# Quartered first loads, high parts kept in PSUM and a paired first output tile in a hybrid decoder step

## The chip, the cores and the metric

The kernel runs on one core of a Trainium2 chip. The metric is the device time of one execution in microseconds (us). Before the change it is 1032.31 us, the median of three runs (1032.12 to 1032.55). Engines are named as in the profile: PE is TensorE (PEld its weight loads), DVE is VectorE, ACT is ScalarE, POOL is GpSimd, SP is SyncE, which here only issues transfers.

## The reference, cut to what matters

One layer of a decoder for 512 prompt rows and 32 sample rows, in float32, D = 1024. The parts around the change:

```
mod = silu(c) @ w_ada + b_ada;  sh1, sc1, g1, sh2, sc2, g2 = split(mod, 6)
u = x * (1 + sc1) + sh1
a = u @ w_in + b_in                       # columns: convolution branch (GLU), q, k, v, two gates
y_conv = conv_branch(glu(a)) ;  y_att = attention(a) @ w_pa + b_pa
y = (gate_c * y_conv + gate_a * y_att) @ w_out + b_out
x = layer_norm(ALPHA * x + (1 + g1) * y, ln1_g, ln1_b)
u = x * (1 + sc2) + sh2 ;  h = (silu(u @ w_gate) * (u @ w_up)) @ w_down
x = layer_norm(ALPHA * x + (1 + g2) * h, ln2_g, ln2_b)
```

c, and so mod, is one vector for the prompt and one for each of 8 sample sequences. The key and value windows and the convolution state are outputs too.

## The kernel before, in words

All 544 columns (512 prompt, 32 sample) stand in the free dimension, in two halves of HC = 272; D lies on the partitions in 8 blocks k. Every float32 product is made of three: an operand is split into a high part (a cast to fp32r, by ACT) and a low part (source minus high, by DVE), and PE adds hi·hi, hi·lo and lo·hi in PSUM. `mm_group` (lines 193 to 205) does this for one 128-column weight tile: 8 blocks x 2 halves x 3 = 48 matmuls of 272 columns, or 24 for one half or for 4 blocks. Its PSUM tiles come from `pmm`, which has four.

Weight tiles come as a stream in a fixed order. `load_more` (L110 to L119) issues their transfers from SP as long as one of four raw buffers `wr` is free; `prep_to` (L121 to L138) splits them (ACT at L133, DVE at L134) into one of three buffers `wh` and `wl`; `w_next` keeps that three tiles ahead of PE. The order on each engine is the order in which the program is written; background generators advance at `tick()`.

**Load phase** (L206 to L321). SP loads the modulation weights `ga` in four groups g of 2 MiB (two transfers each), x in two, and whole tiles of `w_in` in between; ACT loads `ct`, `cst` and `vec`. For each g, `ada_mm(g)` makes the part of sh1 and sc1 that belongs to the blocks k = 2g and 2g + 1 (32 matmuls), `make_u(g)` transposes it, makes modT (DVE, L267) and from it the two blocks of u, split (ACT L274 and L246, DVE L275, L277 and L247, POOL L279 and L280). `early_mm(g)` adds those two blocks' share into the first NE = 3 projection tiles, 36 matmuls, 12 per tile. The written order is product 0, u 0, product 1, u 1, early 0, product 2, u 2, early 1, product 3, u 3, early 2, early 3; the three tiles are split whole in between. Then `mm_group` runs for the further tiles, from 47.2 us.

**Modulation for the rest** (`ada_gen`, L326 to L361): eight blocks `gb` of `w_ada`, loaded by POOL with `ada_load`, are used one after each projection group, the first behind the group m = 3.

**Merge** (L826 to L850). For each of the 8 blocks m, PE makes att @ w_pa (24 matmuls); DVE adds the bias and multiplies by the gate, half by half (L836); for m < DM = 7 POOL adds the convolution branch `t1` (L845), and the split of that block into M is done one step later by `merge_split`; for m = 7 DVE adds (L838) and the split follows at once:

```
act.copy(out=M[h][:, 0, m], in_=mg[:, h * HC:(h + 1) * HC])
dve.tensor_tensor(out=M[h][:, 1, m], in0=mg[:, ...], in1=M[h][:, 0, m].bitcast(F32), op=ALU.subtract)
```

**Output projection and first layer norm** (L980 to L1008). For half h = 0 and then 1, and for the 8 blocks m, `mm_group` multiplies M[h] by `w_out` tile m (`wo`), and DVE adds the result, times 1 + g1, into z (L992). z is x, loaded again by SP (L853); ahead of that first use POOL scales all of it by ALPHA and adds (1 + g1)·b_out (`xbb`) in eight instructions of 512 columns and one for the samples (L989, L991). `Stats` adds sums (DVE) and squares (ACT, added by POOL) as the blocks come; `ln1_gen(h)` finishes the norm between the next matmul groups.

Of the kernel before, what the change touches and what calls it, by code (L numbers as in the profile page):

```python
# [7 lines left out]
F32 = mybir.dt.float32  # L8
# [9 lines left out]
NP = 512  # L18
# [36 lines left out]
def hybrid_step_kernel(ctx: ExitStack, tc: tile.TileContext, I, O):  # L55
# [156 lines left out]
    x_sb = big_tile(2, [128, 8, NT], F32, "x_sb")  # L212
    act.dma_start(out=cst[:, :128], in_=I["cst"][:, :128])
    act.dma_start(out=vec, in_=I["vec"])
    ga = []
    for g in range(4):
        t = big_tile(3 + g, [128, 8, 512], F32, f"ga{g}")
        for i in range(2):
            sp.dma_start(out=t[:, 4 * i:4 * i + 4], in_=I["w_ada0"][g, :, 4 * i:4 * i + 4])
        if g % 2 == 0:  # L220
            sp.dma_start(out=x_sb[:, 2 * g:2 * g + 4], in_=I["x_t"][:, 2 * g:2 * g + 4])
        if g < 2:
            load_more(1 + 2 * g)
        ga.append(t)
    load_more()
    act.dma_start(out=cst[:, 128:], in_=I["cst"][:, 128:])
    dve.memset(cpad, 0.0)
    dve.memset(ones, 1.0)
    dve.memset(epst, EPS)
    pool.memset(smv, 0.0)  # L230
    ident = C("ident")
# [48 lines left out]
        pool.tensor_tensor(out=samp(us), in0=samp(us), in1=bc(modT[:, 0, ks, 1:9]), op=ALU.add)  # L280
        split_samp(us, U[1], ks)

    NE = 3
    early = [[(pmm if m < 2 else ps_s).tile([128, 512], F32, tag="mm" if m < 2 else "s", name="mm") for _ in range(2)] for m in range(NE)]
    ew = []

    def early_mm(g):
        for m in range(NE):
            hi, lo = ew[m]
            for k in (2 * g, 2 * g + 1):  # L290
                for h in range(2):
# [6 lines left out]
    a0 = ada_mm(0)
    make_u(0, a0)
    prep_to(1)  # L300
    a1 = ada_mm(1)
    prep_to(2)
    make_u(1, a1)
    prep_to(3)
    for m in range(NE):
        ew.append(preps.pop(m))
    pos["use"] = NE
    early_mm(0)
    a2 = ada_mm(2)
    make_u(2, a2)  # L310
    early_mm(1)
    a3 = ada_mm(3)
    make_u(3, a3)
    early_mm(2)
    dve.tensor_scalar(out=qb, in0=V("b_in", 0, 60), scalar1=0.125, scalar2=None, op0=ALU.mult)


    aslots = (3, 4, 5, 6, 3, 4, 6, 4)
    abox = {}

    def ada_load(c):  # L321
        t = big_tile(aslots[c], [128, 2, 2048], F32, f"gb{c}")
        pool.dma_start(out=t, in_=I["w_ada12"][c])
        abox[c] = t

    def ada_gen():  # L326
# [35 lines left out]
    glu_p = glu[:, :4 * 542].rearrange("p (c t) -> p c t", c=4)  # L362
    glu_s = glu[:, 4 * 542:4 * 542 + 4 * NB * 34].rearrange("p (c b t) -> p c b t", c=4, b=NB)
    ctmp = glu[:, 4 * 542 + 4 * NB * 34:].rearrange("p (b t w) -> p b t w", b=NB, w=CW)
    for c in range(4):
        ada_load(c)
    pool.memset(glu_p[:, :, 0:30], 0.0)
    for c in range(4):
        pool.dma_start(out=glu_s[:, c, :, 0:30], in_=I["state"][:, c])
# [455 lines left out]


    def merge_split(m, mg, h):
        act.copy(out=M[h][:, 0, m], in_=mg[:, h * HC:(h + 1) * HC])
        dve.tensor_tensor(out=M[h][:, 1, m], in0=mg[:, h * HC:(h + 1) * HC], in1=M[h][:, 0, m].bitcast(F32), op=ALU.subtract)  # L829

    for m in range(8):
        ps = mm_group(w_next(), att, 4)
# [146 lines left out]
    for h in range(2):  # L979
        stats = Stats(h, dve)  # L980
        for m in range(8):
            if h == 0:
                wo.append(w_next())
            ps = mm_group(wo[m], M, 8, halves=(h,))[h]
            n1 = HC if h == 0 else 240
            zz = stats.zt(m)
            if h == 0 and m == 0:
                for k in range(8):
                    pool.tensor_scalar(out=z[:, k, :NP], in0=z[:, k, :NP], scalar1=ALPHA, scalar2=xbb[:, k:k + 1], op0=ALU.mult, op1=ALU.add)  # L989
                prep_to(pos["use"] + XP)  # L990
# [510 lines left out]
```

## Time and profile before

| | before |
|---|---|
| median of three runs | 1032.31 us (1032.12 to 1032.55) |
| the profiled execution | 1033.35 us |
| its span, first to last instruction | 1031.6 us |
| mean granted PE clock | 0.986 |
| PE / PEld busy | 985.8 us (96%) / 942.2 us (91%) |
| DVE / ACT / POOL busy | 652.1 us (63%) / 479.7 us (47%) / 236.3 us (23%) |
| moved by DMA | 242.64 MB, mean 235 GB/s |

The page gives busy times by engine and by 40 slices of the span; matmuls are pipelined, so a busy PE is not PE at its peak, and start-to-start distances tell more than single durations. Further views: stretches (busy time of each engine between two times, with the granted clock and the DMA engines' share), the timeline (instructions in order of time, with the idle time before them and what ended it), lines or tiles (min, median and max of one kind of instruction), the list of waits, and the DMA view.

### The profile page before, as it was taken

Reading aid. Unit: us, or ns where it says so; the run is one execution under the profiler, and the core shown is the slowest. Engines: PE = TensorE matmul, PEld = TensorE weight load, DVE = VectorE, ACT = ScalarE, POOL = GpSimd, SP = SyncE. Lnnn points to the kernel's source line nnn. Section 1 sums busy time; section 2 is a strip of 40 time slices with the busy share of each in tenths; the row PEclk is TensorE's granted clock in tenths of the full one; section 3 lists DMA queues with packets and bytes.
Section 4 is the critical chain, followed back from the end, with each engine's and each line's share of the span. In section 5 each row is a group of like instructions: output and inputs, shape, how many; then the busy total and the mean of one; then the engine's idle time right before and its main releaser. Section 6 shows DMA issues by size and latency. Waiting matters only on the chain.

```text
span 1031.6 us, 21539 instructions
## 1 busy us (share of the span) xinstructions
PE 985.8 (96%) x8964; PEld 942.2 (91%) x8964; DVE 652.1 (63%) x1156; ACT 479.7 (47%) x931; POOL 236.3 (23%) x279
## 2 busy tenths in 40 slices
PE   4999999999999999999999998989999999999995
PEld 3887999999998999999999998989999999999994
DVE  3422788879886654342217887687546875578687
ACT  3312235545447667534433445656325652266333
POOL 0301010010013310101103444054014440344046
PEclk8999999999999999999999998999999999999998
DMA  9998687696784674699953620124964769565612
GB/s 379 361 385 319 244 298 261 246 339 233 277 324 163 238 271 154 236 378 384 367 202 99 242 83 21 42 83 170 349 255 162 266 209 360 205 246 207 213 50 86
DMA packets 44945, 242.64 MB, mean 235 GB/s; under 512 B 7408, under 2 KB 10736, under 8 KB 37680
## 3 DMA queue, kind: packets, MB, share of 16 engines
q1 hardware_dynamic: 34592, 126.83, 34.4%
q10 hardware_dynamic: 7632, 88.43, 23.0%
q0 software_dynamic: 2624, 26.02, 6.3%
q8 instruction: 70, 1.15, 0.4%
q14 instruction: 27, 0.22, 0.1%
HBM read 231.36 MB, written 97.58 MB: 319 GB/s over the span
## 4 chain that ended last, share of the span: by engine, by line
PE 61%; DVE 12%; issue 8%; ACT 7%; POOL 6%; DMA 5%; ACTq 0%; DVEq 0%; POOLq 0%
PE mm L199 15%; PE mm L200 14%; PE mm L202 14%; POOL ss L1077 4%; DMA wr<-in_w_gu 3%; PE od L740 2%; PE mm L1120 2%; PE Sd L705 2%; PE mm L1121 2%; PE mm L1122 2%; PE adaps L334 1%; DVE mrg L829 1%; DMA wr<-in_w_in 1%; PE pt L516 1%; DVE wl L134 1%
## 5 line engine op out<-in xcount | busy, mean ns | idle before, releaser
L199 PE MATMUL mm<-u,wh 128*128 128x272 f32 x1016 | 283.4, 296 | 1.2 <-ACT wh L133 0.9
L200 PE MATMUL mm<-u,wh 128*128 128x272 f32 x1016 | 275.6, 289 | 0.0
L202 PE MATMUL mm<-u,wl 128*128 128x272 f32 x1016 | 213.2, 290 | 1.3 <-DVE wl L134 1.2
L199 PEld LDWEIGHTS mm<-u,wh 128*128 128x128 f32 x1016 | 192.4, 189 | 15.8 <-issue 11.4
L200 PEld LDWEIGHTS mm<-u,wh 128*128 128x128 f32 x1016 | 192.7, 190 | 0.3
L134 DVE TENSOR_TENSOR wl<-wr,wh 128x1024 fp32r<-128x1024 f32 (+2 forms) x100 | 117.5, 1176 | 86.5 <-ACT wh L133 86.5
L202 PEld LDWEIGHTS mm<-u,wl 128*128 128x128 f32 x1016 | 160.4, 189 | 1.9 <-DVE wl L134 1.9
L133 ACT CAST wh<-wr 128x1024 fp32r<-128x1024 f32 (+2 forms) x100 | 97.0, 972 | 64.6 <-PE mm L200 50.5
L439 DVE SCALAR_TENSOR_TENSOR convy<-glu,vec,convy 128x512 f32<-128x512 f32 x120 | 95.7, 797 | 2.5
L1077 POOL TENSOR_TENSOR ss<-wr 128x512 f32<-128x512 f32 x34 | 50.6, 1487 | 189.3 <-DVE s L1104 85.9
L200 PE MATMUL mm<-h,wh 128*128 128x272 f32 x240 | 64.7, 288 | 0.0
L199 PE MATMUL mm<-h,wh 128*128 128x272 f32 x240 | 64.5, 286 | 0.0
L1034 DVE SCALAR_TENSOR_TENSOR z<-mm,modT,z 128x272 f32<-128x272 f32 (+1 forms) x48 | 21.7, 479 | 49.0 <-PE mm L202 49.0
L637 ACT ACTIVATE qk<-mm,vec 128x272 f32<-128x272 f32 (+1 forms) x48 | 25.9, 627 | 56.5 <-PE mm L202 56.5
L202 PE MATMUL mm<-h,wl 128*128 128x272 f32 x240 | 49.6, 288 | 0.0
L1093 ACT CAST wh<-ss 128x512 fp32r<-128x512 f32 (+1 forms) x34 | 28.4, 835 | 42.8 <-POOL ss L1077 32.1
L199 PEld LDWEIGHTS mm<-h,wh 128*128 128x128 f32 x240 | 45.2, 188 | 0.0
L200 PEld LDWEIGHTS mm<-h,wh 128*128 128x128 f32 x240 | 45.1, 188 | 0.0
L1120 PE MATMUL mm<-ta,wh 128*128 128x272 f32 x136 | 40.4, 297 | 4.6 <-DVE wg L1142 4.6
L509 ACT ACTIVATE P<-P,st 128x256 f32<-128x256 f32 x64 | 31.2, 488 | 28.2 <-DVE st L503 25.7
L654 POOL DMA_DIRECT2D out_kv<-qk x4 | 2.4, 597 | 182.5 <-ACT qk L637 182.5
L200 PE MATMUL mm<-mrg,wo 128*128 128x272 f32 x128 | 37.8, 296 | 1.8 <-DVE mrg L829 1.7
(329 smaller groups left out, 2545.4 us busy)
## 6 DMA issues: line engine op xcount, KB each, us to landing
out_s<-in_c ACTq DMA_DIRECT2D x32, 2044.0 KB, 10.4
wr<-in_w_in SPq DMA_DIRECT2D x60, 512.0 KB, 6.6
wr<-in_w_gu SPq DMA_DIRECT2D x44, 512.0 KB, 3.8
KT<-in_kt SPq DMA_DIRECT2D x24, 792.0 KB, 7.9
VV<-in_vv SPq DMA_DIRECT2D x24, 768.0 KB, 7.8
gb<-in_w_ada POOLq DMA_DIRECT2D x8, 2048.0 KB, 16.9
out_s<-in_c ACTq DMA_DIRECT2D x8, 2032.0 KB, 10.1
ga<-in_w_ada SPq DMA_DIRECT2D x8, 1024.0 KB, 14.3
```

What stands on the lines that cost most here:

```text
L133: act.copy(out=hv, in_=raw)
L134: dve.tensor_tensor(out=lv, in0=raw, in1=hv.bitcast(F32), op=ALU.subtract)
L199: pe.matmul(ps[h][:, :HC], lhsT=hi[:, k], rhs=A[h][:, 0, k], start=(k == 0), stop=False)
L200: pe.matmul(ps[h][:, :HC], lhsT=hi[:, k], rhs=A[h][:, 1, k], start=False, stop=False)
L202: pe.matmul(ps[h][:, :HC], lhsT=lo[:, k], rhs=A[h][:, 0, k], start=False, stop=(k == nk - 1))
L439: dve.scalar_tensor_tensor(out=o, in0=src, scalar=sc, in1=o, op0=ALU.mult, op1=ALU.add)
L509: act.activation(out=p[:, a:b], in_=p[:, a:b], func=AF.Exp, bias=st[:, kd, s, hh, 0:1], accum_out=st[:, kd, s, hh, 1:2])
L637: act.activation(out=o, in_=src, func=AF.Identity, bias=V("b_in", col))
L1034: dve.scalar_tensor_tensor(out=zz[:, :n1], in0=ps[:, :n1], scalar=modT[:, 5, m, 0:1], in1=zz[:, :n1], op0=ALU.mult, op1=ALU.add)
L1077: pool.tensor_tensor(out=o, in0=x, in1=y, op=op)
L1093: act.copy(out=hi, in_=src_of(f, n))
L1120: pe.matmul(ps[:, :HC], lhsT=hi[:, k], rhs=B[:, 0, k], start=(first and k == 0), stop=False, skip_group_check=not first)
```

## The change

1. **Load phase.** x comes in four transfers and the first three `w_in` tiles in quarters (two blocks k each), so that SP loads for each g: `ga`, x, three quarters. The quarters are split one by one (`prep_quarters`), and the early matmuls are spread: `early_mm` takes a list of tiles. Twelve, later six matmuls of `ones` by `ones` (`warm`) are put ahead. The rest of `cst` is loaded by SP behind these.
2. **Modulation for the rest.** Its first four `gb` are loaded by SP instead of POOL, two at once and two behind the groups m = 3 and 4; the products start one group later.
3. **Merge.** For m < 7 ACT copies the high part once more, into a PSUM tile (`mhi`), and DVE subtracts that copy.
4. **Output projection.** The first two tiles of half 0 share one loop: blocks k = 0 to 5 of both, then 6 and 7 of both. z is scaled by ACT block by block, one block ahead of its use, instead of by POOL at once.

```diff
+    def ga_load(g):
+        for i in range(2):
+            sp.dma_start(out=ga[g][:, 4 * i:4 * i + 4], in_=I["w_ada0"][g, :, 4 * i:4 * i + 4])
+    def x_load(g):
+        sp.dma_start(out=x_sb[:, 2 * g:2 * g + 2], in_=I["x_t"][:, 2 * g:2 * g + 2])
+    def w_quarters(g):
+        for m in range(NE):
+            sp.dma_start(out=eraw[m][:, 2 * g:2 * g + 2], in_=stream[m][0][:, 2 * g:2 * g + 2])
+    NE = 3
+    eraw = [wrp.tile([128, 8, 128], F32, tag="wr", name="wr") for _ in range(NE)]
     for g in range(4):
...
+        ga_load(g)
+        x_load(g)
+        w_quarters(g)
+    pos.update(load=NE, prep=NE, use=NE)
     load_more()
-    act.dma_start(out=cst[:, 128:], in_=I["cst"][:, 128:])
+    sp.dma_start(out=cst[:, 128:], in_=I["cst"][:, 128:])
...
+    def warm(n):
+        t = ps_t.tile([128, 128], F32, tag="t", name="warm")
+        for _ in range(n):
+            pe.matmul(t, lhsT=ones, rhs=ones, start=True, stop=True)
+    def prep_quarters(g):
+        ks = slice(2 * g, 2 * g + 2)
         for m in range(NE):
+            hi, lo = ew[m]
+            act.copy(out=hi[:, ks], in_=eraw[m][:, ks])
+            dve.tensor_tensor(out=lo[:, ks], in0=eraw[m][:, ks], in1=hi[:, ks].bitcast(F32), op=ALU.subtract)
+            done[m] = g == 3
+        load_more()
...
+    warm(12)
+    make_u(0, ada_mm(0))
+    prep_quarters(0)
+    warm(6)
+    early_mm(0, (0, 1))
+    make_u(1, ada_mm(1))
+    prep_quarters(1)
+    early_mm(0, (2,))
+    early_mm(1, (0,))
+    make_u(2, ada_mm(2))
+    prep_quarters(2)
+    early_mm(1, (1, 2))
+    early_mm(2, (0,))
+    make_u(3, ada_mm(3))
+    prep_quarters(3)
+    early_mm(2, (1, 2))
...
-    for c in range(4):
-        ada_load(c)
+    for c in range(2):
+        ada_load(c, sp)
...
-        next(ada12, None)
+        if m > NE:
+            next(ada12, None)
+        if m < NE + 2:
+            ada_load(m - NE + 2, sp)
...
     def merge_split(m, mg, h):
+        hi = M[h][:, 0, m].bitcast(F32)
         act.copy(out=M[h][:, 0, m], in_=mg[:, h * HC:(h + 1) * HC])
-        dve.tensor_tensor(out=M[h][:, 1, m], in0=mg[:, h * HC:(h + 1) * HC], in1=M[h][:, 0, m].bitcast(F32), op=ALU.subtract)
+        if m < DM:
+            seen = ps_s.tile([128, 512], F32, tag="s", name="mhi")[:, :HC]
+            act.copy(out=seen, in_=hi)
+            hi = seen
+        dve.tensor_tensor(out=M[h][:, 1, m], in0=mg[:, h * HC:(h + 1) * HC], in1=hi, op=ALU.subtract)
...
-            if h == 0:
+            if h == 0 and m == 0:
+                wo.extend((w_next(), w_next()))
+                pair = [pmm.tile([128, 512], F32, tag="mm", name="mm") for _ in range(2)]
+                for ks in (range(6), (6, 7)):
+                    for i in range(2):
+                        for k in ks:
+                            pe.matmul(pair[i][:, :HC], lhsT=wo[i][0][:, k], rhs=M[0][:, 0, k], start=(k == 0), stop=False)
+                            pe.matmul(pair[i][:, :HC], lhsT=wo[i][0][:, k], rhs=M[0][:, 1, k], start=False, stop=False)
+                            pe.matmul(pair[i][:, :HC], lhsT=wo[i][1][:, k], rhs=M[0][:, 0, k], start=False, stop=(k == 7))
+            elif h == 0 and m > 1:
                 wo.append(w_next())
...
-            if h == 0 and m == 0:
-                for k in range(8):
-                    pool.tensor_scalar(out=z[:, k, :NP], in0=z[:, k, :NP], scalar1=ALPHA, scalar2=xbb[:, k:k + 1], op0=ALU.mult, op1=ALU.add)
-                prep_to(pos["use"] + XP)
-                pool.tensor_scalar(out=z[:, :, NP:], in0=z[:, :, NP:], scalar1=ALPHA, scalar2=None, op0=ALU.mult)
+            if h == 0 and m < 7:
+                for k in ((0, 1) if m == 0 else (m + 1,)):
+                    act.activation(out=z[:, k, :NP], in_=z[:, k, :NP], func=AF.Identity, scale=ALPHA, bias=xbb[:, k:k + 1])
+            if h == 0 and m == 6:
+                act.activation(out=z[:, :, NP:], in_=z[:, :, NP:], func=AF.Copy, scale=ALPHA)
```

How it moves instructions, at three places. On SP at the start of the program (`ga` modulation weights, `wr` raw weight tiles, `gb` the later modulation weights, `cst` constants), before:

```order
L219 DMA ga_111<-in_w_ada 128x2048 x2
L221 DMA x_sb<-in_x_t 128x2176
L117 DMA wr<-in_w_in 128x1024
L219 DMA ga_117<-in_w_ada 128x2048 x2
L117 DMA wr<-in_w_in 128x1024 x2
L219 DMA ga_124<-in_w_ada 128x2048 x2
L221 DMA x_sb<-in_x_t 128x2176
L219 DMA ga_128<-in_w_ada 128x2048 x2
L117 DMA wr<-in_w_in 128x1024 x26
```

and now:

```order
L219 DMA ga_111<-in_w_ada 128x2048 x2
L222 DMA x_sb<-in_x_t 128x1088
L226 DMA wr<-in_w_in 128x256 x3
L219 DMA ga_112<-in_w_ada 128x2048 x2
L222 DMA x_sb<-in_x_t 128x1088
L226 DMA wr<-in_w_in 128x256 x3
L117 DMA wr<-in_w_in 128x1024
L236 DMA cst<-in_cst 128x940
L346 DMA gb_549<-in_w_ada 128x4096
L117 DMA wr<-in_w_in 128x1024 x3
L346 DMA gb_551<-in_w_ada 128x4096
```

The tiles that SP loaded whole now come in three pieces behind each group of `ga` and x (the second and third such groups, which read alike, are left out here), the constants have come over from ACT, and two blocks of `gb` stand ahead of and among the next weight tiles.

On ACT in the load phase, from one copy of a modulation product (`modsb`) to the next (`u` the split input, `wh` high parts of weights), before:

```order
L262 COPY modsb<-adaps 128x128
L274 ACTIVATE u_140<-x_sb,modT 128x272
L274 ACTIVATE u_141<-x_sb,modT 128x240
L246 CAST u_141<-us 128x2x32
L133 CAST wh<-wr 128x1024 x2
L262 COPY modsb<-adaps 128x128
```

and now:

```order
L272 COPY modsb<-adaps 128x128
L284 ACTIVATE u_151<-x_sb,modT 128x272
L284 ACTIVATE u_152<-x_sb,modT 128x240
L256 CAST u_152<-us 128x2x32
L306 CAST wh<-wr 128x256 x3
L272 COPY modsb<-adaps 128x128
```

The two whole tiles split ahead of the next product (of the four parts of u two are shown) have become three quarters, and this now repeats for each of the four groups.

On ACT at the end of the merge (`mrg` the high parts of M, `mhi` their copies in PSUM, `wo` the output projection's weights, `lnq` squares of the layer norm), before:

```order
L133 CAST wo_6346<-wr 128x1024
L828 CAST mrg_6348<-mg 128x272
L828 CAST mrg_6349<-mg 128x272
L828 CAST mrg_6348<-mg 128x272
L828 CAST mrg_6349<-mg 128x272
L133 CAST wo_6346<-wr 128x1024 x2
L133 CAST wo_6681<-wr 128x1024 x3
L898 ACTIVATE lnq<-z 128x272
```

and now:

```order
L133 CAST wo_6395<-wr 128x1024
L855 CAST mrg_6397<-mg 128x272
L858 COPY mhi<-mrg_6397 128x272
L855 CAST mrg_6398<-mg 128x272
L858 COPY mhi<-mrg_6398 128x272
L855 CAST mrg_6397<-mg 128x272
L855 CAST mrg_6398<-mg 128x272
L133 CAST wo_6395<-wr 128x1024 x2
L1029 ACTIVATE z<-z,xbb 128x512 x3
L133 CAST wo_6758<-wr 128x1024
L1029 ACTIVATE z<-z,xbb 128x512
```

Each deferred split has a copy behind its cast, and the scaling of z, which POOL did in one run, stands among the casts of the `w_out` tiles. On PE the first 48 matmuls of the output projection stay neighbours; the blocks 6 and 7 of the first tile now come behind blocks 0 to 5 of the second.

## Rows read from the trace of the kernel before

**Rows 1.** Stretches of the load phase: us, busy of each engine (x count), PEclk, DMA share, GB/s.

```profile
16.50:23.00 6.50, 5.38 (x71) 4.40 (x72) 1.70 (x5) 1.47 (x3) 0.22 (x1) 0.50 1.03 417
...
28.40:47.20 18.80, 17.92 (x240) 17.21 (x239) 8.18 (x23) 6.78 (x15) 7.76 (x13) 1.00 0.87 339
```

**Rows 2.** Timeline, load phase: start us, us, engine, line, what, xcount [idle before <-releaser].

```profile
8.46 1.22 PEld L256 LDWEIGHTS adaps<-ga,cpad 128*32 128x32 f32 x32 [0.47 <-DMA ga<-in_w_ada]
...
11.84 0.26 DVE L267 SCALAR_TENSOR_TENSOR modT<-modt,vec 128x18 f32<-128x18 f32 x2 [5.38 <-DMA vec<-in_vec]
...
16.57 1.94 PE L256 MATMUL adaps<-ga,cpad 128*32 128x128 f32 x32 [5.89 <-DMA ga<-in_w_ada]
...
18.97 1.94 PE L256 MATMUL adaps<-ga,cpad 128*32 128x128 f32 x32 [0.47 <-DMA ga<-in_w_ada]
```

**Rows 3.** Timeline of PE at the first output projection groups.

```profile
569.90 0.29 PE L199 MATMUL mm<-mrg,wo 128*128 128x272 f32 x1
...
572.18 0.29 PE L199 MATMUL mm<-mrg,wo 128*128 128x272 f32 x1
...
574.19 0.39 PE L200 MATMUL mm<-mrg,wo 128*128 128x272 f32 x1 [1.73 <-DVE mrg L829]
...
582.81 0.29 PE L199 MATMUL mm<-mrg,wo 128*128 128x272 f32 x1
```

**Rows 4.** Stretches behind the merge and in the first layer norm.

```profile
576.00:579.40 3.40, 3.40 (x17) 3.40 (x16) 2.68 (x3) 3.40 (x5) 1.51 (x1) 0.50 1.02 397
...
635.30:640.90 5.60, 5.60 (x26) 5.48 (x25) 5.42 (x7) 0.82 (x2) 4.57 (x5) 0.51 0.37 97
```

**Rows 5.** List of waits, PE, 545 to 660 us: us in total, times, longest.

```profile
PE lnps L924 <- DVE lns L881: 1.7, 1, 1.7
PE lnps L925 <- POOL lnq L882: 1.5, 1, 1.5
```

**Rows 6.** DMA view, 0 to 36 us: queue, kind: packets, MB, share of 16 engines.

```profile
q1 hardware_dynamic: 2147, 13.22, 90.8%
...
q10 hardware_dynamic: 576, 0.74, 5.6%
```

**Rows 7.** Timeline, load phase, from the second modT to the end.

```profile
22.45 0.25 DVE L267 SCALAR_TENSOR_TENSOR modT<-modt,vec 128x18 f32<-128x18 f32 x2
...
22.74 2.08 ACT L274 ACTIVATE u<-x_sb,modT 128x272 fp32r<-128x272 f32 x4 [1.30 <-DVE modT L267]
...
25.52 0.22 DVE L247 TENSOR_TENSOR u<-us,u 128x64 fp32r<-128x64 f32 x1
...
28.42 1.95 PE L256 MATMUL adaps<-ga,cpad 128*32 128x128 f32 x64
...
31.18 0.26 DVE L267 SCALAR_TENSOR_TENSOR modT<-modt,vec 128x18 f32<-128x18 f32 x2 [4.02 <-PE modt L264]
...
46.94 0.42 PE L296 MATMUL mm<-u,wl 128*128 128x272 f32 x2
```

**Rows 8.** The merge's tile and line L133: ns min/median/max, first and last start us, forms.

```profile
L828 ACT CAST mrg<-mg x16: 413/418/423, 551.7 to 575.8; 128x272 fp32r<-128x272 f32 x16
...
L829 DVE TENSOR_TENSOR mrg<-mg,mrg x16: 423/436/1608, 552.8 to 576.2; 128x272 fp32r<-128x272 f32 x16
...
L133 ACT CAST wh<-wr x100: 602/1044/1094, 14.2 to 957.9; 128x1024 fp32r<-128x1024 f32 x76, 128x512 fp32r<-128x512 f32 x16, 128x896 fp32r<-128x896 f32 x8
```

**Rows 9.** Timeline of DVE at the end of the merge.

```profile
568.99 0.90 DVE L836 SCALAR_TENSOR_TENSOR mg<-mm,vec,ga 128x272 f32<-128x272 f32 x2
...
572.82 0.49 DVE L836 SCALAR_TENSOR_TENSOR mg<-mm,vec,ga 128x272 f32<-128x272 f32 x1
...
577.16 2.36 DVE L134 TENSOR_TENSOR wo<-wr,wo 128x1024 fp32r<-128x1024 f32 x2 [0.50 <-ACT wo L133]
```

**Rows 10.** Line L1104, its second operand in SBUF or in PSUM (`hip`).

```profile
L1104 DVE TENSOR_TENSOR wl<-wr,wh x37: 677/684/1782, 677.7 to 953.5; 128x512 fp32r<-128x512 f32 x37
...
L1104 DVE TENSOR_TENSOR wl<-ss,hip x14: 686/687/690, 692.2 to 945.6; 128x512 fp32r<-128x512 f32 x14
```

More of the change, by code (lines that the diff above doesn't have):

```diff
@@ L214, in hybrid_step_kernel @@
     act.dma_start(out=vec, in_=I["vec"])
-    ga = []
-    for g in range(4):
[L217 to L224, printed above, removed]
+    ga = [big_tile(3 + g, [128, 8, 512], F32, f"ga{g}") for g in range(4)]
+    def ga_load(g):
[8 more added lines that the diff above has]
+    eraw = [wrp.tile([128, 8, 128], F32, tag="wr", name="wr") for _ in range(NE)]
+    for g in range(4):
+        ga_load(g)
+        x_load(g)
+        w_quarters(g)
+    pos.update(load=NE, prep=NE, use=NE)
     load_more()
-    act.dma_start(out=cst[:, 128:], in_=I["cst"][:, 128:])
+    sp.dma_start(out=cst[:, 128:], in_=I["cst"][:, 128:])
+    dve.memset(ones, 1.0)
     dve.memset(cpad, 0.0)
-    dve.memset(ones, 1.0)
     dve.memset(epst, EPS)
@@ L281, in make_u, with early_mm @@
         split_samp(us, U[1], ks)
-    NE = 3
     early = [[(pmm if m < 2 else ps_s).tile([128, 512], F32, tag="mm" if m < 2 else "s", name="mm") for _ in range(2)] for m in range(NE)]
-    ew = []
-    def early_mm(g):
-        for m in range(NE):
+    def warm(n):
+        t = ps_t.tile([128, 128], F32, tag="t", name="warm")
+        for _ in range(n):
+            pe.matmul(t, lhsT=ones, rhs=ones, start=True, stop=True)
+    ew = [(whp.tile([128, 8, 128], F32R, tag="wh", name="wh"), wlp.tile([128, 8, 128], F32R, tag="wl", name="wl")) for _ in range(NE)]
+    def prep_quarters(g):
+        ks = slice(2 * g, 2 * g + 2)
+        for m in range(NE):
+            hi, lo = ew[m]
[3 more added lines that the diff above has]
+        load_more()
+    def early_mm(g, ms=range(NE)):
+        for m in ms:
             hi, lo = ew[m]
@@ L296, in early_mm @@
                     pe.matmul(early[m][h][:, :HC], lhsT=lo[:, k], rhs=U[h][:, 0, k], start=False, stop=(k == 7))
[L298 to L314, printed above, removed]
+    warm(12)
[14 more added lines that the diff above has]
+    early_mm(2, (1, 2))
     dve.tensor_scalar(out=qb, in0=V("b_in", 0, 60), scalar1=0.125, scalar2=None, op0=ALU.mult)
@@ L319, in hybrid_step_kernel, with ada_load @@
     abox = {}
-    def ada_load(c):
+    def ada_load(c, eng=pool):
         t = big_tile(aslots[c], [128, 2, 2048], F32, f"gb{c}")
-        pool.dma_start(out=t, in_=I["w_ada12"][c])
+        eng.dma_start(out=t, in_=I["w_ada12"][c])
         abox[c] = t
@@ L981, in hybrid_step_kernel @@
         for m in range(8):
-            if h == 0:
+            if h == 0 and m == 0:
[8 more added lines that the diff above has]
+            elif h == 0 and m > 1:
                 wo.append(w_next())
-            ps = mm_group(wo[m], M, 8, halves=(h,))[h]
+            ps = pair[m] if h == 0 and m < 2 else mm_group(wo[m], M, 8, halves=(h,))[h]
             n1 = HC if h == 0 else 240
             zz = stats.zt(m)
-            if h == 0 and m == 0:
-                for k in range(8):
-                    pool.tensor_scalar(out=z[:, k, :NP], in0=z[:, k, :NP], scalar1=ALPHA, scalar2=xbb[:, k:k + 1], op0=ALU.mult, op1=ALU.add)
-                prep_to(pos["use"] + XP)
-                pool.tensor_scalar(out=z[:, :, NP:], in0=z[:, :, NP:], scalar1=ALPHA, scalar2=None, op0=ALU.mult)
+            if h == 0 and m < 7:
[3 more added lines that the diff above has]
+                act.activation(out=z[:, :, NP:], in_=z[:, :, NP:], func=AF.Copy, scale=ALPHA)
             dve.scalar_tensor_tensor(out=zz[:, :n1], in0=ps[:, :n1], scalar=modT[:, 2, m, 0:1], in1=zz[:, :n1],
```

## The prediction

> **What bounds the kernel now.** [...]
>
> The first is the load phase, up to the first full projection group at 47.2 us. From 16.5 to 23.0 us PE is granted 0.50 of its clock while the DMA engines are full; from 28.4 to 47.2 it has no gap to speak of [rows 1]. The reader should see in the timeline what it waited for: the second modulation product sat idle 5.89 us for its weights, its second half came at 18.97, and before that the first modT waited until 11.84 for `vec` [rows 2]. So by 28.4 us little of the three early tiles was done, and the rest had to be worked off after the loads.
>
> The second is the step from the merge to the output projection. PE starts the first `w_out` group at 569.90, issues 18 matmuls, starts the 19th at 572.18 and the 20th only at 574.19; the fourth group starts at 582.81 [rows 3]. From 576.0 to 579.4 the granted clock is 0.50 [rows 4], behind that stall. [...]
>
> After that PE waits twice in the first layer norm, 1.7 us on DVE and 1.5 us on POOL [rows 5], and runs at 0.51 from 635.3 to 640.9 [rows 4]. The change does not address that.
>
> **Load phase: bytes.** A quarter is 2.10 MB of modulation weights, 0.56 MB of x and three pieces of 0.13 MB. Anchor: when the second `ga` ended at 18.97 [rows 2], 6.57 MB had been asked for (two `ga`, half of x, one weight tile, the constants), and the engines moved 0.417 MB per us [rows 1]. In the new order the second `ga` is complete at 5.4 MB, so about 16.2; the third at 8.45 MB, 23.5; the fourth at 11.5 MB, 30.8. Small packets cost more per byte: the queue with short rows spent 5.6% of 16 engines and 36 us on 576 packets, 56 ns each for 1.3 KB, the other 244 ns for 6.2 KB [rows 6]. By these, 1536 packets of 1 KB take some 5.4 us against 3.9 for the same bytes in long rows; I put the fourth `ga` at 31.3 us (30.8 to 32.3).
>
> **Load phase: the chain.** Each quarter now runs modT, U, the quarters' split, early matmuls, next modulation product. From modT at 22.45: ACT's four parts of U end at 24.82, the cast of the sample columns 0.23 behind, one copy of 128x256 about 0.42 (the 128x272 cast of [rows 8]), so the first high part stands at +2.95; DVE's last low part of U ends at 25.74, and one low part of 0.44 behind it stands at +3.7 [rows 7]. PE does four of the twelve matmuls meanwhile and the other eight in 1.0: +4.75. From the start of a modulation product to the next modT is 31.18 - 28.42 = 2.76 [rows 7]. Cycle: 7.5 us.
> Without the wait for `vec` the first modT could come at 10.5 (the second half of the first product ends at 8.46 + 1.22, and the way to modT behind a product is 2.76 - 1.95 = 0.8), with it at 11.84 as before [rows 2, 7]; the x transfer beside which `vec`'s rows are dealt has half the packet length now, so I take 10.9. The first quarter does two tiles, 20 matmuls behind +3.7: +6.25, next modT 10.9 + 6.25 + 2.76 = 19.9, then 27.4 and 34.9. Its products need `ga` at 17.2, 24.6 and 32.1: just behind the arrivals. Behind the last modT come 24 matmuls of the third quarter (3.05), then 36: high part in place, low part at +3.7, 32 left at 0.127: +7.8, 42.7 us. Before it was 47.2: 4.5 us gained at full clock.
> That PE is at full clock at 13.9 us is not sure. Warm-up matmuls (12, then 6) stand where PE was idle, up to 6.5 us. A modulation product is 32 matmuls, four side by side, in 1.95 [rows 7], 0.24 for each four; a warm-up moves as many columns, so it costs 0.24, or 0.49 at the lower level, and 12 are done before the product can start. In the trace PE began at 6.5; the 32 weight loads that began at 8.46 took 1.22, where 64 take 1.69 at full clock, so the level rose some 2.8 us after the first work; on the second occasion, from 16.6, it had not risen by 23.0 [rows 1, 2, 7]. I take 2.8 us: from 13.85 to 16.65 twelve matmuls at 0.227 instead of 0.127, 1.1 us lost. **Term: 3.4 us** (bounds: 4.7 with `vec` early and full clock throughout; 1.8 if the level rises 6.4 us after 13.85).
> At nothing, with cover: `cst` to SP's tail (first used in attention); the later modulation loads, which now stand in SP's queue among the weight tiles. The fourth to sixth weight tiles are issued behind 2.1 MB only when the last quarter is split (38.6 us), land at 42 to 45 and are first needed 6 us behind 42.7; the modulation product c = 0 moves one group later. If that cover went, PE would wait for what is missing, 1.2 us per late tile.
>
> **Merge and output projection.** DVE lags: the seventh group's eviction starts at 568.99, the last at 572.82, 3.83 apart, where PE delivers every 24 x 0.127 = 3.04 [rows 9]. In each step one of the two subtractions takes 1608 ns instead of 436, because both operands lie in SBUF while POOL adds [rows 8]. With the high part in PSUM the subtraction took 687 for 512 elements, with both in SBUF 684 at the median but up to 1782; the former ran beside POOL's adds of the same line's operands, and none took more than 690 [rows 10]. So 1.17 us of waiting go, but the weight split that follows still reads SBUF twice and meets the rest of POOL's add, some 0.8: each step gets 0.3 to 0.4 shorter. Steps with 4-block weights then keep up with PE; the two with `w_out` splits do not. The last eviction comes 1.9 us earlier by this; I take 1.5 (bounds 0 and 2.9, the whole lag).
> ACT pays 14 copies of 0.42: with two casts of 0.42 and a weight cast of 1.04 that is 2.7 us in a step of 3.04 [rows 8], nothing on the path.
> [...]
> PE: the first six blocks of two tiles are 36 matmuls, 569.90 to 574.5; the stalled low part is then there (574.19 before, earlier now), the last twelve end at 576.0. No stall, so no fall of the clock. The third tile's low part was ready at 577.16 + 1.2 = 578.4 [rows 9], now 576.9: PE does two matmuls and waits 0.7; 22 x 0.127 later the third group ends at 579.7 where it ended at 582.81. **Term: 3.1 us** (bounds 1.6, DVE no earlier, and 3.75, no wait).
> z's prescale leaves POOL for ACT: eight activations of 0.6 to 1.04 (ACT's four parts of U take 2.08 for 1024 elements with scale and bias [rows 7]), one per group of 3.04 us, beside a cast of 1.04 [rows 8]: at nothing. POOL's prescale had no one waiting on PE's side. If ACT came late, the squares for the layer norm would be late next.
>
> **Sum.** 3.4 + 3.1 = 6.5. The profiled execution took 1033.35 us for a span of 1031.6: 1026.85. It lies 1.04 above the median 1032.31, so I forecast 1032.3 - 6.5 = 1025.8; the two terms' bounds give 1023.9 to 1028.9.
>
> **The rivals.**
> *The gain at the merge is waited away in the layer norm.* PE's waits there name DVE and POOL [rows 5]; were that chain bound by its own work, PE would come 3.1 us earlier and wait 3.1 us longer: 1028.9. Against: before 582.8 DVE waits for PE's groups, so the chain moves with them.
> *The level stays at half to 23 us, as now.* Then 24 matmuls cost 5.45, the second modulation product 1.75 more, the end is 46.7: 0.5 + 3.1, 1028.7. For: the gaps between early matmuls remain. Against: PE works from 1 us on.
> *The half-clock stretch at 635 goes too.* 5.6 us at half cost 2.8: 1023.0.
> *It does nothing:* PE's in-order queue makes each product wait for the split of the quarter before, and the arrivals slip: 1031 to 1032.3.
> *Slower:* one mechanism, PE's level in the load phase. Its work is now spread thinly over 40 us; if every gap keeps it at half, the cycle is 3.7 + 1.8 + 4.7 = 10.2, with 5.45 instead of 3.05 for the 24 matmuls of one quarter and 8.2 for the last 36 the phase ends near 60 instead of 47.2: 12.8 - 3.1 = 9.7 slower, 1042. It is slower than before once 44% of the phase (42.7 to 60.0, break-even 50.3) is at half. For: the level fell after one short burst [rows 1, 2]. Against: at half PE would hardly idle.
> [...]
>
> **How the numbers follow.** Forecast with its bounds 0.55; layer norm 0.14; half to 23 us 0.10; stretch at 635 goes 0.08; nothing 0.08; slower 0.05. The range 1023.0 to 1029.5 takes in the first four, 0.87. A measurement of this kernel tells 0.2%, 2.1 us, from no change: faster 0.87, same 0.08, slower 0.05.
>
> **What would show it.** Right: first full group at 43 to 45 us; modT at about 11, 21, 28 and 36; subtractions of the merge all near 0.44; no matmul of the first pair waiting; granted clock 1.00 from 570 to 630; a wait under 1 us at the third `w_out` tile. Wrong: that group at 47 or later, a clock of 0.50 past 20 us, PE's waits in the layer norm grown by 3 us, or `ga` named as what PE waits for at 30 us.

## The result, and the profile after

The changed kernel took 1026.32 us in the median of 4 runs (1025.97 to 1026.41) beside 1032.43 us for the kernel before (median of 4, 1032.12 to 1034.87): ratio 0.9929, 95% interval 0.9914 to 0.9944. By the medians that is 6.1 us less where 6.5 were forecast. The profiled execution took 1026.41 us for a span of 1024.2, against 1033.35 and 1031.6.

**Load phase.** The stretches view of after, columns as in [rows 1]:

```profile
8.50:16.00 7.50, 5.42 (x62) 4.61 (x63) 4.05 (x12) 3.40 (x9) 0.66 (x2) 1.00 1.04 407
16.00:23.00 7.00, 5.22 (x89) 4.58 (x88) 2.96 (x9) 3.17 (x9) 0.66 (x2) 1.00 1.02 407
```

The granted clock is 1.00 where [rows 1] had 0.50. The timeline of PE, load phase of after:

```profile
1.06 4.69 PE L298 MATMUL warm<-ones 128*128 128x128 f32 x24 [1.06 <-DVE ones L237]
...
8.58 1.08 PE L266 MATMUL adaps<-ga,cpad 128*32 128x128 f32 x32 [0.88 <-DMA ga<-in_w_ada]
...
22.67 0.39 PE L317 MATMUL mm<-u,wh 128*128 128x272 f32 x1 [1.39 <-ACT wh L306]
...
32.33 1.95 PE L266 MATMUL adaps<-ga,cpad 128*32 128x128 f32 x64
...
42.92 0.29 PE L199 MATMUL mm<-u,wh 128*128 128x272 f32 x1
```

The 5.89 us for the second `ga` [rows 2] are gone, and the last modulation product (32.33) waits for nothing. The first full group starts at 42.92, 4.28 earlier. The modT rows of DVE's timeline set the beat:

```profile
10.70 0.26 DVE L277 SCALAR_TENSOR_TENSOR modT<-modt,vec 128x18 f32<-128x18 f32 x2 [4.14 <-DMA vec<-in_vec]
...
19.80 0.26 DVE L277 SCALAR_TENSOR_TENSOR modT<-modt,vec 128x18 f32<-128x18 f32 x2 [4.81 <-PE modt L274]
...
27.44 0.26 DVE L277 SCALAR_TENSOR_TENSOR modT<-modt,vec 128x18 f32<-128x18 f32 x2 [3.34 <-PE modt L274]
...
35.09 0.26 DVE L277 SCALAR_TENSOR_TENSOR modT<-modt,vec 128x18 f32<-128x18 f32 x2 [3.35 <-PE modt L274]
```

Not all of the 4.28 us lasts: at 380.46 in before, 376.51 in after, the same transposes of `fb` are 3.95 apart. PE's timeline shows one of the takers, which before had not:

```profile
79.45 1.92 PE L357 MATMUL adaps<-gb,cpad 128*32 128x512 f32 x16 [0.21 <-DMA gb<-in_w_ada]
```

**Merge and output projection.** The same view, later:

```profile
565.95 0.29 PE L1019 MATMUL mm<-mrg,wo 128*128 128x272 f32 x1
...
571.99 0.29 PE L199 MATMUL mm<-mrg,wo 128*128 128x272 f32 x1
572.12 0.29 PE L200 MATMUL mm<-mrg,wo 128*128 128x272 f32 x1
572.54 0.40 PE L202 MATMUL mm<-mrg,wo 128*128 128x272 f32 x1
...
575.43 0.29 PE L199 MATMUL mm<-mrg,wo 128*128 128x272 f32 x1
```

The pair's 48 matmuls run through. The third tile waits for its low weights: two starts 0.42 apart instead of 0.127, so 0.3 us. The fourth group starts 582.81 - 575.43 = 7.38 us earlier than before [rows 3], the first 569.90 - 565.95 = 3.95: the merge gives 3.43. DVE, in the tile view and the timeline:

```profile
L860 DVE TENSOR_TENSOR mrg<-mg,mhi x14: 422/430/439, 548.9 to 568.2; 128x272 fp32r<-128x272 f32 x14
```

```profile
554.03 0.91 DVE L867 SCALAR_TENSOR_TENSOR mg<-mm,vec,ga 128x272 f32<-128x272 f32 x2
554.85 0.78 DVE L860 TENSOR_TENSOR mrg<-mg,mhi 128x272 fp32r<-128x272 f32 x2
555.70 1.31 DVE L134 TENSOR_TENSOR wl<-wr,wh 128x512 fp32r<-128x512 f32 x1
557.03 0.91 DVE L867 SCALAR_TENSOR_TENSOR mg<-mm,vec,ga 128x272 f32<-128x272 f32 x2
...
566.92 0.49 DVE L867 SCALAR_TENSOR_TENSOR mg<-mm,vec,ga 128x272 f32<-128x272 f32 x1
```

No deferred subtraction takes 1608 ns any more [rows 8]. The weight split takes the wait in its place (1.31 us), and the step, from one L867 to the next, is 3.00 us, PE's own. Only the two steps with splits of `w_out` tiles are longer, 3.46 and 3.43 us. The last eviction starts 0.97 us behind the first output matmul, before 2.92 [rows 3, 9].

**Layer norm.** The list of waits, PE, 560 to 665 us, and the stretches that run at half clock in after:

```profile
PE lnps L955 <- DVE lns L912: 1.7, 1, 1.7
PE lnps L956 <- POOL lnq L913: 1.5, 1, 1.5
PE mm L199 <- ACT wh L133: 1.2, 1, 1.2
```

```profile
308.60:311.90 3.30, 3.30 (x14) 3.07 (x14) 1.81 (x3) 1.44 (x6) 0.00 (x0) 0.50 0.77 248
626.00:632.80 6.80, 5.54 (x22) 5.31 (x23) 5.34 (x6) 2.34 (x5) 5.14 (x5) 0.50 0.28 80
687.50:690.80 3.30, 3.30 (x16) 3.30 (x15) 2.83 (x6) 1.54 (x4) 0.00 (x0) 0.50 0.08 22
```

Both waits are those of [rows 5], and the stretch of [rows 4] is there, with 0.50 from 625.99 on instead of 633.99. The other two are not in the trace of before.

### The profile page after: what moved, and what is told of

It reads as the page before. It is cut to its first block, busy times and chain, and to the rows that moved or that the text cites. A ratio compares the mean times of both kernels' runs of the same rounds, so it can differ in the third digit from the quotient of the medians.

```text
span 1024.2 us, 21677 instructions
## 1 busy us (share of the span) xinstructions
PE 990.5 (97%) x9000; PEld 947.0 (92%) x9000; DVE 651.1 (64%) x1165; ACT 492.3 (48%) x963; POOL 221.7 (22%) x266
## 4 chain that ended last, share of the span: by engine, by line
PE 59%; DVE 12%; ACT 8%; issue 8%; DMA 7%; POOL 5%; ACTq 0%; POOLq 0%; DVEq 0%; SPq 0%
PE mm L199 14%; PE mm L200 14%; PE mm L202 13%; POOL ss L1117 3%; DMA wr<-in_w_gu 3%; DMA gb<-in_w_ada 3%; PE mm L1160 2%; PE mm L1162 2%; PE mm L1161 2%; PE od L766 2%; PE Sd L731 2%; DVE wl L134 1%; PE pt L542 1%; PE adaps L357 1%; DMA wr<-in_w_in 1%
## 5 line engine op out<-in xcount | busy, mean ns | idle before, releaser
L133 ACT CAST wh<-wr 128x1024 fp32r<-128x1024 f32 (+2 forms) x97 | 93.9, 969 | 53.8 <-PE mm L200 42.7
L1162 PE MATMUL mm<-ta,wl 128*128 128x272 f32 x136 | 39.5, 290 | 0.0
```

Of the source, the lines that this page charges most:

```text
L133: act.copy(out=hv, in_=raw)
L1162: pe.matmul(ps[:, :HC], lhsT=lo[:, k], rhs=B[:, 0, k], start=False, stop=(k == 3), skip_group_check=not first)
```

## The experiments

The kernel before took 1032.4 us in the first comparison and 1033.2 to 1033.4 in those that follow, so each run is read by its ratio to the kernel before, by its trace, and by its median beside those of the runs of one comparison: e1 to e4; e0 and e5 to e7; e8 and e9; e10 and e11. The interval of a ratio reaches some 1.3 us to either side. A difference of medians between two comparisons is weaker than one within a comparison.

### One part at a time

e1 is the kernel before with the load phase's hunks alone, e2 with those of the merge and the output projection alone.

> The kernel before with the load phase's part of the change alone (quarters, warm-ups, the later modulation loads on SP); merge and output projection as before. In the profiled pair PE's lead was 4.0 us from 120 us on and 7.4 us behind the merge, but the medians differ by 6.1 only. Theory A: the two parts add up and the lead read in the pair is right, so load alone gives 4.0: 1028.4 us, first full group at 42.9, the wait of 1.7 us on mrg at the first output projection group still there. Theory B (the missing 1.3 us is in the load part): 1029.7. Theory C (the parts overlap, a PE that comes earlier is held up later without the other part): 1030 or more, with the wait on mrg longer than 1.73 us.

> The kernel before with the merge's high parts in PSUM, the paired output tiles and z's prescale on ACT alone; load phase as before. Theory A: 3.4 us of lead as in the profiled pair less what the profiled execution of before had too much, that is the stretch at half clock behind the stall, which other executions may not have: 1030.0 us (6.1 - 4.0 = 2.1 less than before), no wait on mrg, first full group at 47.2. Theory B: 1029.0 (the whole 3.4). Theory C (overlap): 1031 or more.

Load alone: 1028.94 us against 1033.34, ratio 0.9958 (0.9945 to 0.9970), 4.4 us. Merge alone: 1029.94, ratio 0.9968 (0.9957 to 0.9980), 3.4 us. For the load this is near theory A. For the merge the gain is theory B's 3.4; the time is theory A's 1030.0 only because the kernel before took 1033.3 here, though A's gain of 2.1 lies just at the edge of the interval. C falls for both. PE's timeline of e1, then its stretches behind the stall and at the layer norm:

```profile
566.10 0.29 PE L199 MATMUL mm<-mrg,wo 128*128 128x272 f32 x1
...
568.37 0.29 PE L199 MATMUL mm<-mrg,wo 128*128 128x272 f32 x1
570.38 0.40 PE L200 MATMUL mm<-mrg,wo 128*128 128x272 f32 x1 [1.73 <-DVE mrg L855]
...
577.50 0.29 PE L199 MATMUL mm<-mrg,wo 128*128 128x272 f32 x1
```

```profile
570.00:576.00 6.00, 5.56 (x42) 5.34 (x43) 4.69 (x8) 4.46 (x6) 1.59 (x1) 1.00 0.94 358
626.00:633.00 7.00, 3.92 (x25) 3.41 (x26) 4.61 (x9) 4.89 (x11) 4.16 (x5) 1.00 0.14 25
...
658.60:662.00 3.40, 3.25 (x14) 2.93 (x14) 2.71 (x6) 0.71 (x2) 0.00 (x0) 0.50 0.38 110
```

The stall of 1.73 us is that of [rows 3], but the level did not fall behind it as in [rows 4]. So in this execution PE is 3.80 us ahead of before at the first output group (566.10), 5.31 at the fourth (577.50), and 4.9 at the end (spans 1026.7 and 1031.6): the load phase itself gives 3.8, the missing fall the rest. This would account for 4.4 and 3.4 making more than the whole change gave beside a kernel before of nearly the same time (6.7, e0 below): e2 counts the fall to the merge, and in e1 it did not come. But the excess, 1.1 us, is no larger than the intervals, and only one execution of each was traced.

### The changed kernel again

> The changed kernel again, beside the three others and the kernel before on one chip. On the chip of the last four runs the kernel before took 1033.34 us, not 1032.43. Theory A (load 4.0 to 4.4, merge 3.4, they add up): the gain there is 7.0 us (6.8 to 7.8), so 0.993 of before; the 6.1 of the first comparison was a matter of which executions of before had the stretch at half clock. Theory B: it stays at 6.1.

1026.53 us against 1033.23, ratio 0.9940 (0.9927 to 0.9952): 6.7 us by the medians, 6.2 by the ratio. That lies between theory A's range and theory B's 6.1 and decides for neither. The profiled execution was the slowest of its five, 1027.47 us. Two rows of it, a stretch and PE's timeline, matter below:

```profile
10.90:14.40 3.50, 3.33 (x15) 3.36 (x16) 3.26 (x10) 3.13 (x8) 0.66 (x2) 0.51 1.02 424
```

```profile
80.64 1.92 PE L357 MATMUL adaps<-gb,cpad 128*32 128x512 f32 x16 [1.34 <-DMA gb<-in_w_ada]
```

### Without the warm-ups

```diff
-    warm(12)
...
-    warm(6)
```

> The changed kernel without the 18 warm-up matmuls. Theory A: they are what puts the granted clock at 1.00 from 4.8 us on; without them it rises only some 2.8 us after PE's first product (6.6), so near 9.4, falls again in the gap behind it as in the kernel before (12.77), and the first quarter's 24 early matmuls and the second modulation product run at half (0.227 instead of 0.127 us each, and 1.75 us more): up to 4.2 us, part of it hidden in PE's wait of 1.4 us at 21: first full group near 45, 1028.5 us (1027.5 to 1030). Rival: PE only waits for data there, the level does not matter: 1026.3, first full group at 43.

1028.44 us, ratio 0.9950 (0.9936 to 0.9964), 1.9 above the changed kernel's 1026.5, and as much above e4 (1026.56, next section), which ran beside it and has the warm-ups; first full group at 44.67. Theory A. The profiled execution was the fastest of its five, 1027.50 us. The stretches of e3:

```profile
4.50:10.70 6.20, 3.87 (x64) 2.74 (x64) 0.23 (x1) 0.43 (x2) 0.00 (x0) 1.00 1.03 402
10.70:14.10 3.40, 0.35 (x2) 0.16 (x2) 2.64 (x8) 2.69 (x8) 0.66 (x2) 1.00 1.03 424
14.20:17.50 3.30, 3.30 (x15) 3.30 (x16) 1.31 (x5) 0.44 (x2) 0.00 (x0) 0.50 0.99 394
```

PE does next to nothing from 10.7 to 14.1, and behind that the early matmuls run at 0.50: from the first of them to the second modulation product PE takes 4.74 us (14.08 to 18.82) instead of 3.53 (13.56 to 17.09). The other half microsecond is lost earlier. The first modT comes at 11.21 instead of 10.70, because the first product ran at the lower pace too, 32 weight loads in 1.48 us where after needs 0.81, although the clock column shows 1.00 from 4.5 on:

```profile
6.59 1.48 PEld L266 LDWEIGHTS adaps<-ga,cpad 128*32 128x32 f32 x32 [6.59 <-DVE cpad L243]
```

So the 1.75 us that the phase is longer are 0.5 in the first product and 1.2 in the early matmuls.

### Pair and copies

e4 takes the pair away, e5 the copies into PSUM, e9 the copies and POOL's adds.

```diff
-                for ks in (range(6), (6, 7)):
...
+            ps = mm_group(wo[m], M, 8, halves=(h,))[h]
```

> The changed kernel with the first two output tiles as two groups, one after the other, as before; high parts still in PSUM. Theory A (the PSUM copies carry the gain): the low parts of the seventh and eighth block are there 2.3 and 3.0 us behind the first output matmul (568.24 and 568.94 against 565.95), PE wants them at 2.4 and 2.8: a wait of 0.2 us, 1026.5 us. Rival (the pair carries it): a wait of 1.7 us and a stretch at half clock behind it as before, 1028.5 to 1029.5.

1026.56 us, ratio 0.9933 (0.9920 to 0.9945), the same as the changed kernel. In PE's timeline the eighth block's second matmul (k = 7) starts 0.34 us behind the first instead of 0.127:

```profile
569.16 0.29 PE L199 MATMUL mm<-mrg,wo 128*128 128x272 f32 x1
569.50 0.39 PE L200 MATMUL mm<-mrg,wo 128*128 128x272 f32 x1
```

That is a wait of 0.2 us, as theory A had it: with the copies there, the pair has little left to hide.

```diff
-        if m < DM:
-            seen = ps_s.tile([128, 512], F32, tag="s", name="mhi")[:, :HC]
-            act.copy(out=seen, in_=hi)
-            hi = seen
```

> The changed kernel without the copies of the high parts into PSUM; the pair stays. Theory A (DVE's lag is what the copies remove): subtractions up to 1.6 us again, the last eviction 1.9 us later; the pair hides the seventh block's low part (ready 4.2 us behind the first output matmul, wanted at 4.6), but the third tile's low weights come 1.9 us later: PE waits about 2 us there, and the level may fall behind it: 1.9 to 3.6 us slower than the changed kernel beside it. Rival (the pair alone is enough): within 0.5 us of it.

1028.95 us, ratio 0.9962 (0.9950 to 0.9975), 2.4 above e0 beside it: theory A. PE's, DVE's and POOL's timelines of e5:

```profile
566.65 0.29 PE L1014 MATMUL mm<-mrg,wo 128*128 128x272 f32 x1
...
578.05 0.29 PE L199 MATMUL mm<-mrg,wo 128*128 128x272 f32 x1
```

```profile
552.85 1.95 DVE L855 TENSOR_TENSOR mrg<-mg,mrg 128x272 fp32r<-128x272 f32 x2
554.72 0.68 DVE L134 TENSOR_TENSOR wl<-wr,wh 128x512 fp32r<-128x512 f32 x1
555.32 0.90 DVE L862 SCALAR_TENSOR_TENSOR mg<-mm,vec,ga 128x272 f32<-128x272 f32 x2
...
558.62 0.90 DVE L862 SCALAR_TENSOR_TENSOR mg<-mm,vec,ga 128x272 f32<-128x272 f32 x2
```

```profile
553.10 1.40 POOL L871 TENSOR_TENSOR mg<-mg,t 128x544 f32<-128x544 f32 x1 [1.89 <-DVE mg L862]
```

From the first output group to the fourth PE takes 11.40 us, exactly as in e1, which has neither pair nor copies; in the changed kernel it is 9.48. The pair removes the stall of 1.73 us, but PE then waits three times for split weights of `w_out` tiles (0.34, 0.45 and 0.74 us), so without the copies the pair gains nothing.

POOL's add ends at 554.50. The two subtractions end at 554.80, so the first ended some 0.43 before that, about with the add. The step is 3.30 us where PE delivers every 3.0. This does not show yet that POOL is the cause:

```diff
-            pool.tensor_tensor(out=mg, in0=mg, in1=t1[:, m], op=ALU.add)
+            dve.tensor_tensor(out=mg, in0=mg, in1=t1[:, m], op=ALU.add)
```

> The changed kernel without the copies into PSUM and with POOL's adds of the merge on DVE: nothing runs on POOL during the merge. Theory A (a DVE subtraction with both operands in SBUF is held until POOL's add of that moment ends): all subtractions 0.43 to 0.44 us and all splits of 512 columns 0.68, none of 1.6; DVE's step is then 0.91 + 0.80 + 0.78 + 0.68 = 3.2 us, against 3.3 without the copies and POOL adding, and 3.0 in the changed kernel; time between those two kernels, 1027 to 1029. Rival (the long ones come from SBUF itself or from ACT's casts): some subtractions stay at 1.6 us and the step is 4 us, over 1030.

1027.35 us, ratio 0.9939 (0.9925 to 0.9952): by the ratio level with e0, in the median 0.8 us above it. The line view of e9, then DVE's and PE's timelines:

```profile
L855 DVE TENSOR_TENSOR mrg<-mg,mrg x16: 433/435/444, 549.8 to 570.5; 128x272 fp32r<-128x272 f32 x16
```

```profile
551.26 0.91 DVE L862 SCALAR_TENSOR_TENSOR mg<-mm,vec,ga 128x272 f32<-128x272 f32 x2
...
554.26 0.91 DVE L862 SCALAR_TENSOR_TENSOR mg<-mm,vec,ga 128x272 f32<-128x272 f32 x2
```

```profile
566.18 0.29 PE L1014 MATMUL mm<-mrg,wo 128*128 128x272 f32 x1
...
575.63 0.29 PE L199 MATMUL mm<-mrg,wo 128*128 128x272 f32 x1
```

Both operands lie in SBUF, POOL is idle, and no subtraction is long: it is POOL's add that holds them, not SBUF and not ACT's casts. DVE does the add in 0.73 us, and its step is 3.00 us, shorter than expected. From the first output group to the fourth e9 takes 9.45 us, beside 9.48 in the changed kernel: here moving the add does as much as the 14 copies. What e9 loses in its profiled execution, it loses elsewhere: it is 7.19 us ahead of before at 625 us (the changed kernel 7.39) and 6.4 at the end (7.4). Why was not traced.

### z's prescale on POOL

```diff
-                    act.activation(out=z[:, k, :NP], in_=z[:, k, :NP], func=AF.Identity, scale=ALPHA, bias=xbb[:, k:k + 1])
+                    pool.tensor_scalar(out=z[:, k, :NP], in0=z[:, k, :NP], scalar1=ALPHA, scalar2=xbb[:, k:k + 1], op0=ALU.mult, op1=ALU.add)
```

> The changed kernel with z's prescale on POOL again, as before. Theory A (no one waits for it): within 0.3 us of the changed kernel. Rival: POOL's eight passes over 512 columns run beside DVE's splits of the third and fourth output tile, which read SBUF twice and then take up to 1.8 us or more instead of 1.23, so PE waits 0.6 us or more at each of them: 1 to 2 us slower.

1026.80 us, ratio 0.9941 (0.9929 to 0.9953): no difference. DVE's work on z waits for POOL's passes four times, 0.2 to 0.7 us each, and the splits of `w_out` tiles beside them stay at 1.2: the move was worth nothing that can be told, as the prediction's step had it.

### What caps the load phase

e7 brings the weight pieces before x from the second quarter on, splits them beside the modulation product, and orders the early matmuls block by block, some of them ahead of a transpose:

```diff
-        x_load(g)
-        w_quarters(g)
+        for load in (x_load, w_quarters) if g == 0 else (w_quarters, x_load):
+            load(g)
...
-    early_mm(1, (0,))
-    make_u(2, ada_mm(2))
-    prep_quarters(2)
...
+    a2 = ada_mm(2)
     prep_quarters(2)
...
+    make_u(2, a2, [(0, 3)])
```

> A version that may beat the changed kernel: from the second quarter on the three weight pieces come before x, so their split runs while PE does the modulation product and modT is followed by U alone; early matmuls go block by block, six of them beside the copy that each transpose waits for. Theory A: PE's wait of 1.4 us at 21 goes, and the phase is bound by the arrival of the last modulation weights (32) and the way from modT to the last low part of U (3.1 us) and 18 matmuls behind it: first full group at 41.1 instead of 42.9, 1.8 us faster than the changed kernel beside it. Rival (x comes too late): PE waits for x from 19 us on, no gain or up to 1 us slower.

1026.78 us, ratio 0.9946 (0.9933 to 0.9960): no gain, but not as the rival has it: what ACT and POOL wait for before they make u is modT each time, not x. The first full group came at 42.19, 0.73 earlier than in the profiled execution of the changed kernel. At the first later modulation product, near 55 us, 0.27 of it was left, and the fourth came at 80.00, 0.55 later than the changed kernel's 79.45. The list of waits of e7, PE, 40 to 130 us, and its stretch with the DMA engines full:

```profile
PE adaps L359 <- DMA gb<-in_w_ada: 1.0, 1, 1.0
```

```profile
34.00:82.00 48.00, 46.07 (x392) 38.49 (x381) 16.42 (x32) 13.20 (x24) 5.67 (x9) 1.00 1.00 396
```

It is the wait that the changed kernel showed with 0.2 us, and e0 with 1.34. e8 is e7 with the later modulation products one group later, and with (1, 5) behind the last product; e10 is the changed kernel with the first of these two edits alone:

```diff
-        if m > NE:
+        if m > NE + 1:
             next(ada12, None)
```

> The version of the last call (weight pieces before x) with the eight later modulation products one group later each, and two early blocks of the third tile behind the last modulation product of the load phase instead of one. In that version the first full group came at 42.2 instead of 42.9, yet at 235 us it was no further than the changed kernel: it lost 0.8 us more on the way, where PE waits 1.0 us (0.2 in the changed kernel) for the modulation load gb at 79 us, while the DMA engines are full from 34 to 82 us. Theory A (that arrival is the next bound): with the products a group later there is no such wait, first full group near 41.5, and 1.2 to 1.7 us less than the changed kernel: 1025.0 us. Rival (the weight stream itself is late): the wait turns up elsewhere between 45 and 100 us, same time as the changed kernel, 1026.5.

> The changed kernel with nothing but the eight later modulation products one group later each. In the traces with the changed load phase PE waits for the modulation load gb near 79 us between 0.2 and 1.3 us (0.2, 1.3, 0.5, 0.8, 0.8, 0.2 and 0.5 in seven of them); without the warm-ups, where the phase ends 1.8 us later, it does not wait. Theory A (that wait caps what the load phase gives): it is gone, first full group at 42.9 as before, and the time is 0.2 to 1.3 us, at the middle 0.6, under the changed kernel's 1026.5: 1025.9. Rival (the products later run into the next tenant of their buffers): no gain or slower.

> The version with weight pieces before x and the products a group later, beside the run above. Theory A: 1024.6 again, 1.3 us under the run above, as much as its first full group comes earlier (41.4 against 42.9, 1.4 us). Rival (its first result was luck with the level's falls): the same time as the run above.

e8: 1024.61 us, ratio 0.9913 (0.9900 to 0.9927); e11: 1024.79, ratio 0.9918 (0.9904 to 0.9931). e10: 1025.75, ratio 0.9927 (0.9914 to 0.9939), first full group at 42.98 and no wait for `gb`: 0.8 us under e0 and 0.6 under the first result, though in another comparison. In e11 that group starts at 41.93, 1.05 earlier than in e10 beside it, and the median is 0.96 less; in the two profiled executions 0.58 of the lead is left at the first later product (60.49 against 61.07) and 0.5 at the end (spans 1023.4 and 1023.9). So the arrival of `gb` was a cap, and with it gone earlier work pays, by the medians nearly in full, in this pair of traces by half. e8 beats both kernels; its median is 1.9 us below the changed one's 1026.5.

## Why the prediction was right, and where it was not

**Load phase, the chain: right.** modT was forecast for 10.9, 19.9, 27.4 and 34.9 at full clock and came at 10.70, 19.80, 27.44 and 35.09; the end at full clock for 42.7, and it was 42.92 (the sign given was 43 to 45).

**Load phase, 1.1 us for the level: wrong.** The step said that from 13.85 to 16.65 twelve matmuls cost 0.227 instead of 0.127 (which makes 1.2 us, not 1.1). In the profiled execution the clock was 1.00 there, behind the warm-ups; without them it was 0.50 from 14.2 to 17.5 (e3). In e0 it was 0.51 from 10.9 to 14.4, and the first full group still started at 42.98: half clock fell for the most part on the six warm-ups (2.90 us instead of 1.57), which stand where PE waits for the first high part anyway, and the early matmuls began at 13.62 instead of 13.56. Only without warm-ups did half clock reach the path (e3). The trace of before has both prices: 0.127 us is (572.18 - 569.90) / 18 [rows 3], and at 0.50 [rows 4] PE's timeline has 14 steps from start to start in 579.19 - 576.02 = 3.17 us, 0.226 each:

```profile
576.02 0.43 PE L199 MATMUL mm<-mrg,wo 128*128 128x272 f32 x1
...
579.19 0.38 PE L202 MATMUL mm<-mrg,wo 128*128 128x272 f32 x1
```

**"At nothing, with cover": wrong for the later modulation loads.** The step put the product c = 0 one group later and saw nobody wait. The fourth of them waits 0.2 to 1.3 us near 79, while the DMA engines' share from 34 to 82 us is 1.00 (after and e7); without that wait the kernel is 0.6 to 0.8 us faster by the medians (e10). The two errors run against each other: the phase ended 0.9 us before the 42.7 + 1.1 of the sum, and of the 4.28 us gained there 3.95 are left at the first output group in after, 3.80 in e1 and 2.90 in e0. That the term of 3.4 lies among these is in part luck.

**Merge: the mechanism right, the size a little short.** Forecast 3.1; 3.43 in the trace and 3.4 in e2. From the first output group to the fourth PE took 12.91 us before, 11.40 in e1 and e5, and 9.48 now. So 1.92 of the 3.43 us are DVE's lag, which the copies remove, and 1.51 the fall of the clock behind the stall, which is not in every execution. The last eviction came 2.92 - 0.97 = 1.95 us earlier, which is the 1.9 of the working and not the 1.5 that I took; hence 0.3 instead of 0.7 us of waiting at the third tile. The operand in PSUM made the subtraction no slower: 430 ns with `mhi`, 435 with both operands in SBUF (e9). The credit goes to the copies (e5: 2.4 us by the medians), not to the pair (e4, and e5 beside e1).

**The rivals.** Waiting the gain away in the layer norm fell: 1.7 and 1.5 us as before. Half clock to 23 us, and slower, fell with the clock of 1.00; e3 shows what was behind the former. "Does nothing" fell. The stretch at 635 stayed (the sign "1.00 from 570 to 630" held up to 625.99), and its price was wrong: in e1 and e5 the clock is 1.00 from 626 to 633, and the list of waits of e1 shows where it goes:

```profile
PE mm L199 <- ACT wh L133: 2.8, 1, 2.8
```

PE comes earlier to the first feed-forward weights and waits 2.8 us for them instead of 1.2, with 0.50 of the clock behind that wait. From the matmul that waits 1.7 us for DVE to the first with `ta`, 55 us on, PE takes 55.57 us before, with the stretch at half clock (632.39 to 687.96), and 55.56 in e1 without it (627.55 to 683.11): the stretch costs nothing there. The forecast of 2.8 us for this rival counted matmuls and not who waits next.

**The base.** The spans of the profiled pair differ by 7.4 us, the medians by 6.1: about 1 because the profiled execution of before lay above its median, and most of the rest because after spends 2.2 us outside its span and before 1.75. So it is in part luck that the medians came within 0.4 us of the forecast gain: the traced pair gave 7.4. Why executions of the kernel before fall near 1032.3, 1033.3 or 1034.9 was not traced.

## What to carry to other kernels

When a phase is shortened, ask which transfer was due just behind its end: here, with the DMA engines' share at 1.00 from 34 to 82 us, the early finish met a wait of 0.2 to 1.3 us for `gb` near 79, and with the consumer one group later that wait was gone (e10). Before an operand is copied to another memory, ask whose work holds the operation up; moving that work can do the same (9.45 us in e9 beside 9.48 with the copies). Price a stretch at half clock by the wait that follows it, not by its matmuls: PE took 55.57 us with the stretch, 55.56 without it (e1).

## What the runs showed of the hardware that was not expected

The level does not fall each time at the same place: behind the same stall of 1.73 us it was 0.50 in before [rows 4] and 1.00 in e1.

Half clock can cost nothing in the end. In after it was 0.50 from 308.60 to 311.90, in before not; yet PE's lead, 4.01 us at the `fb` transposes ahead of it (306.21 against 310.22), is still 3.95 at those behind it and at the group at 565.95.

A DVE operation with both operands in SBUF was held for about as long as POOL's add lasted: 1.6 us instead of 0.43 beside an add of 1.40. With one operand in PSUM it was not held (439 ns at most), and the next operation with two in SBUF was (1.31 instead of 0.68).
